# Moving a small gate's chain of work to an earlier stage, and storing residual rows to DRAM so that the last stage works in natural row order

## The chip, the cores and the metric

The kernel runs on one core of one Trainium2 chip. The metric is device time in microseconds (us) of one execution; the time of a kernel is the median of its runs. The engines are named as in the profile: PE (TensorE, matmuls), PEld (its weight loads, which overlap matmuls), DVE (VectorE), ACT (ScalarE), POOL (GpSimd), and SP (SyncE, which here only issues DMAs). Each engine works through its own instructions in order; semaphores order them against each other. "L208" is line 208 of the kernel.

## The reference

One layer of a streaming encoder over 512 rows ("tokens") of 1024 channels, in float32. Cut to what is computed:

```python
h = rms_norm(x, mix_norm_pre)
xa, ga, q, k, v, f_logit, g_a, g_b = split(h @ w_in)     # widths 1280 1280 1024 1024 1024 16 1024 1024
y_a = gelu(ga) * rg_lru(causal_dwconv4(xa))              # gated linear recurrence along the rows
cum = cumsum(log_sigmoid(f_logit + b_forget))            # the forget gate: one number per head and row
y_b = causal softmax(q k^T / 8 + cum_i - cum_j) @ v      # 16 heads of 64
merged = sigmoid(g_a + b0) * (y_a @ w_proj_a) + sigmoid(g_b + b1) * (y_b @ w_proj_b)
x = x + rms_norm(merged @ w_out, mix_norm_post)          # the residual rows
h = rms_norm(x, ffn_norm_pre)
u = causal_dwconv3(h @ w_up)                             # 6144 channels: gate and value halves
return x + rms_norm((gelu(u_gate) * u_val) @ w_down, ffn_norm_post)
```

The forget gate is a small part of it: 16 columns of the input projection, a log-sigmoid, and a running sum along the rows, of which the attention needs -8 times the sum as a bias for its keys.

## The kernel before

Every float32 operand of a matmul is split into a high part, rounded to the format in which PE multiplies at speed, and a low remainder; a product is three matmuls (high by high, high by low, low by high). So each weight tile of 128 partitions takes a DMA load into `raw`, a cast on ACT into `wh` (L205) and a subtraction on DVE into `wl` (L208). `raw`, `wh` and `wl` have four slots each. Activations are split in the same way.

The stages, in the order in which PE runs them, are: the projection xa with the gates of the recurrence; v in two halves (`v0`, `v1`, four weight tiles each); ga (ten tiles); pa, which multiplies the recurrent branch by w_proj_a in sixteen steps (L907 to L917); q0 and k0; the merge gates ma and mb, by a scheme with seven products in place of eight for a pair of tiles; the attention with the remaining q and k; pb; w_out (`wo`) with the two norms; the up projection by the same seven-product scheme; and the down projection by another one, in 42 steps of twelve matmuls.

What sets the order: a planner walks each engine's instructions by program order, and lets a later one go first where the earlier one isn't ready. `issue_after` ties instructions behind a named one on the same engine. Under `manual_schedule` (the gates, the up and down projections) the program's own order is kept. So v, ga, pa and the w_out stage are ordered by the planner, and the down projection by hand.

The pieces that the change touches, and those beside them:

- **The helper `background`** (L180): after each weight tile of the early stages, POOL copies one element of that weight into `tick` (L182) and then issues DMAs that prepare sums of the down weights. The copy reads `wh`, so that slot comes free only when the copy is done.
- **`forget`** (L836) is called in pa step 3 (L878). It loads w_f (L841), splits it on ACT and DVE (L844, L845), runs sixteen matmuls over all tokens into `pf` (L848, L849), and then works on 16 partitions by 512 columns: the copy of the low part (L851), the sum with the bias (L852), the log-sigmoid (`log1p_exp_neg`, L303: one Exp on ACT, then a series on DVE with seven multiply-adds at L315), the running sum (L860) and the scaled keys (L862). Four DMAs on SP's queue store the keys to the DRAM tile `cnd` (L864), from which the attention's bias is broadcast (L950). Its tiles come from the pool of the recurrence's `tt` tiles.
- **`early_sums`** (L876) is called after each pa step. From step 3 on the pools of the recurrence are closed; steps 6 to 11 compute sums of token halves `hf` (eight DVE operations of 128x1024, L887 to L893); step 12 loads the first pair of gate weights; steps 13 to 15 compute and split their sums (`gt`, `gth`, `gtl`).
- **The start of the gates** (L963 to L991): ACT casts the four `hf` into `gsh` (L967), DVE subtracts into `gsl`, then the weights of the first pair are split, the products p12 and p5 run, and `p.keep(2)` and `p.add` (L468, L480) have to be done before the next product.
- **The residual rows**: `x2t` holds x with 128 rows on partitions, 4 x 1024 values each. The host lays the rows of each block of 128 out so that the 64 even rows come first, then the 64 odd ones. `mix_norm` (L1225) adds the normed w_out output to `x2t` (L1240), squares it on ACT (L1242), takes the root (L270), scales it into `xn` (L1248) and hands it to PE for transposition (L294).
- **The down projection**: step i uses a weight tile (`wd[i]`) and a block of y, which `y_hi` (L1450) casts on ACT into `ah` and `y_lo` (L1456) subtracts on DVE into `al`. `tokens(..., parted)` reads every second column of y, and `placed` writes them side by side, so that the output rows come in the even-then-odd order of `x2t`. Later blocks of y are combined on DVE before (`q`, L1563). `prep(i)` is the order in which a step's four splits are issued; `extra` holds what is to be done beside a step.
- **The end**: blocks t = 2, 3 of the output are finished by a DMA that adds `x2t` (L1621), blocks 0 and 1 on DVE (L1615); the host reorders the rows of the result (L1784).

Of the kernel before, what the change touches and what calls it, by code (L numbers as in the profile page):

```python
# [8 lines left out]
F32 = mybir.dt.float32  # L9
# [3 lines left out]
ALU = mybir.AluOpType  # L13
# [84 lines left out]
def kernel(  # L98
# [432 lines left out]
    with ExitStack() as rg:  # L531
# [275 lines left out]

        v_out(0, pv)
        pv = v_start(1)
        for u in range(4):  # L810
            w = unit(f"v1_{u}")
            v_mm(u, pv, w)
            background(1, w)
            for t in range(5 * u // 2, 5 * (u + 1) // 2):
                batch([rg_tanh(t), rg_exp(t)])
                inflow(t)
        v_out(1, pv)
        steps = {0: (range(0, 4), ()), 1: (range(4, TR), range(0, 2)), 2: ((), range(2, 5)), 3: ((), range(5, 7)), 4: ((), range(7, 9)), 5: ((), range(9, TR))}
# [15 lines left out]
        cnd = ctx.enter_context(tc.tile_pool(name="cnd", bufs=1, space=bass.MemoryType.DRAM)).tile([H, PO[NT]], F32, name="cnd")  # L834

        def forget():  # L836
            def tl(name, n=H, dt=F32):
                return tpool.tile([P, S], dt, tag="tt", name=f"f_{name}")[0:n]

            fr = tl("fr", P)[:, : KD * H].rearrange("p (k e) -> p k e", k=KD)  # L840
            nc.sync.dma_start(fr, w_f)  # L841
            fw = tl("fw", P, F32R)[:, : KD * 48].rearrange("p (k e) -> p k e", k=KD)
            pool.memset(fw[:, :, H:32].bitcast(F32), 0.0)
            act.copy(fw[:, :, 0:H], fr)  # L844
            dve.tensor_tensor(out=fw[:, :, 32:48], in0=fr, in1=fw[:, :, 0:H].bitcast(F32), op=ALU.subtract)  # L845
            pf = bank("f")
            for k in range(KD):
                pe.matmul(pf[0:48], fw[:, k], turns(hh[:, k]), start=k == 0, stop=False)  # L848
                pe.matmul(pf[0:48], fw[:, k], turns(hl[:, k]), start=False, stop=k == KD - 1)  # L849
            z = tl("z")  # L850
            act.copy(z, pf[32:48])  # L851
            dve.scalar_tensor_tensor(out=z, in0=pf[0:H], scalar=cpt[0:H, C_BF : C_BF + 1], in1=z, op0=ALU.add, op1=ALU.add)  # L852
            with tc.issue_after(last_act[0].ins):
                l1p = log1p_exp_neg(z, tl)
            dve.tensor_scalar(out=z, in0=z, scalar1=0.0, scalar2=None, op0=ALU.min)
# [930 lines left out]
```

## Time and profile before

| | us |
|---|---|
| median of 3 runs | 884.94 (884.58 to 885.01) |
| the profiled execution | 884.92 |
| its span, first to last instruction | 883.1 |
| busy: PE, DVE, ACT, POOL | 868.6, 743.5, 608.4, 236.3 |

The profile is of one execution. Its span leaves out about 1.8 us around the first and last instruction. The granted clock of PE was 0.998 of full speed. Where the stages lie in the span, from the first matmul of each: ga from 126.5 us, pa from 178.3, q0 from 233.5, the gates from 245.0, the down projection from 760.0.

A row of the page's groups, or of the lines view, reads: line, engine, operation, output <- inputs, shapes, count | busy us, mean ns of one | idle time of the engine before it, and what ended that. A row of the timeline reads: start in us, duration, engine, line, operation, and in brackets the idle time before it and its releaser. A row of the waits view reads: who waited <- for whom: total us, how many times, the longest. A row of the windows view reads: stretch, its length, busy us of each engine shown with the number of instructions, the clock, the share of time that the DMA engines were busy, and GB/s. "q" behind an engine's name is its sequencer, which issues DMAs.

### The profile page before, as it was taken

Reading aid. Unit: us, or ns where it says so; the run is one execution under the profiler, and the core shown is the slowest. Engines: PE = TensorE matmul, PEld = TensorE weight load, DVE = VectorE, ACT = ScalarE, POOL = GpSimd, SP = SyncE. Lnnn points to the kernel's source line nnn. Section 1 sums busy time; section 2 is a strip of 40 time slices with the busy share of each in tenths; the row PEclk is TensorE's granted clock in tenths of the full one; section 3 lists DMA queues with packets and bytes.
Section 4 is the critical chain, followed back from the end, with each engine's and each line's share of the span. In section 5 each row is a group of like instructions: output and inputs, shape, how many; then the busy total and the mean of one; then the engine's idle time right before and its main releaser. Section 6 shows DMA issues by size and latency. Waiting matters only on the chain.

```text
span 883.1 us, 15782 instructions
## 1 busy us (share of the span) xinstructions
PE 868.6 (98%) x5856; PEld 792.3 (90%) x5856; DVE 743.5 (84%) x1209; ACT 608.4 (69%) x1031; POOL 236.3 (27%) x283
## 2 busy tenths in 40 slices
PE   9999999999999999999999999999999999999996
PEld 7888888888899998888888889999999999888884
DVE  8986479637978849998868599999999999889997
ACT  7565695532466648776754597888888888688774
POOL 4244344535411024232205100242332332100000
PEclk9999999999999999999999999999999999999999
DMA  7787689999865477453506762879899898699864
GB/s 269 242 288 207 188 214 265 227 273 196 190 148 165 120 261 274 133 173 127 203 26 203 234 200 95 192 178 241 210 222 240 209 233 210 230 384 303 280 192 147
DMA packets 71040, 185.24 MB, mean 210 GB/s; under 512 B 7153, under 2 KB 27681, under 8 KB 70578
## 3 DMA queue, kind: packets, MB, share of 16 engines
q1 hardware_dynamic: 47360, 127.72, 43.4%
q0 software_dynamic: 23456, 56.37, 29.8%
q8 instruction: 46, 0.75, 0.3%
q14 instruction: 32, 0.26, 0.1%
q10 hardware_dynamic: 146, 0.14, 0.0%
HBM read 150.69 MB, written 35.73 MB: 211 GB/s over the span
## 4 chain that ended last, share of the span: by engine, by line
PE 83%; DVE 8%; issue 4%; ACT 2%; POOL 2%; DMA 1%; DVEq 0%; ACTq 0%; POOLq 0%
PE up L464 7%; PE up L462 7%; PE up L461 7%; PE dn L1490 2%; PE dn L1488 2%; PE dn L1489 2%; PE ga L252 2%; PE ga L251 2%; PE ga L253 2%; DVE al L357 2%; PE pb L251 2%; PE xa L251 2%; PE v L341 2%; PE xa L253 2%; PE v L342 2%
## 5 line engine op out<-in xcount | busy, mean ns | idle before, releaser
L397 POOL DMA_DIRECT2D ml<-raw_up x42 | 36.1, 859 | 147.6 <-ACT ml L396 82.5
L1360 DVE SCALAR_TENSOR_TENSOR u<-up,cpt,u 128x511 f32<-128x511 f32 x96 | 71.3, 745 | 3.5 <-ACT u L1354 1.8
L1490 PE MATMUL dn<-wh_dn,al 128*128 128x512 f32 (+1 forms) x180 | 66.6, 370 | 1.3 <-DVE al L357 0.7
L1489 PE MATMUL dn<-wl_dn,ah 128*128 128x512 f32 (+1 forms) x180 | 66.1, 367 | 0.5 <-DVE wl_dn L208 0.5
L1488 PE MATMUL dn<-wh_dn,ah 128*128 128x512 f32 (+1 forms) x180 | 65.8, 366 | 0.2 <-ACT ah L1454 0.2
L461 PE MATMUL up<-sh,th 128*128 128x256 f32 x252 | 59.5, 275 | 0.0
L462 PE MATMUL up<-sl,th 128*128 128x256 f32 x252 | 59.5, 275 | 0.0
L208 DVE TENSOR_TENSOR wl_dn<-raw_dn,wh_dn 128x1024 fp32r<-128x1024 f32 x42 | 52.9, 1259 | 5.4 <-ACT wh_dn L205 5.2
L357 DVE TENSOR_TENSOR tl<-t,th 128x1024 fp32r<-128x1024 f32 x42 | 51.1, 1218 | 0.0
L1354 ACT ACTIVATE u<-up,cpt 128x512 f32<-128x512 f32 x48 | 37.0, 778 | 20.1 <-PE up L464 10.0
L205 ACT CAST wh_dn<-raw_dn 128x1024 fp32r<-128x1024 f32 x42 | 44.4, 1058 | 6.1 <-PE dn L1490 3.7
L461 PEld LDWEIGHTS up<-sh,th 128*128 128x128 f32 x252 | 48.4, 192 | 0.0
L462 PEld LDWEIGHTS up<-sl,th 128*128 128x128 f32 x252 | 48.4, 192 | 0.0
L1368 POOL TENSOR_TENSOR yf<-u,u 128x512 f32<-128x512 f32 x23 | 30.5, 1328 | 59.3 <-issue 46.5
L443 ACT CAST th<-t 128x1024 fp32r<-128x1024 f32 x42 | 43.8, 1044 | 2.4
L1490 PEld LDWEIGHTS dn<-wh_dn,al 128*128 128x128 f32 x180 | 34.1, 189 | 8.0 <-DVE al L357 4.1
L955 POOL TENSOR_TENSOR B<-B,mask 128x128 f32<-128x128 f32 x64 | 30.6, 506 | 34.8 <-DMA B<-cnd 33.7
L461 PE MATMUL up<-h2h,mh 128*128 128x256 f32 x168 | 39.7, 275 | 0.0
L462 PE MATMUL up<-h2l,mh 128*128 128x256 f32 x168 | 39.7, 275 | 0.0
L1489 PEld LDWEIGHTS dn<-wl_dn,ah 128*128 128x128 f32 x180 | 34.1, 189 | 5.8 <-DVE wl_dn L208 1.8
L1050 ACT ACTIVATE P<-P,mx 128x384 f32<-128x384 f32 (+3 forms) x64 | 35.2, 552 | 5.3 <-DVE mx L1045 4.3
L464 PE MATMUL up<-sh,tl 128*128 128x256 f32 x252 | 38.4, 275 | 0.0
(731 smaller groups left out, 3252.4 us busy)
## 6 DMA issues: line engine op xcount, KB each, us to landing
raw_up<-in_w_up_dram SPq DMA_DIRECT2D x48, 512.0 KB, 5.5
td<-in_w_down_dram POOLq DMA_DIRECT2D x36, 512.0 KB, 6.3
raw_dn<-td SPq DMA_DIRECT2D x24, 512.0 KB, 5.4
ml<-raw_up POOLq DMA_DIRECT2D x21, 512.0 KB, 5.4
B<-cnd POOLq DMA_DIRECT2D x16, 640.0 KB, 5.7
raw_dn<-in_w_down_dram SPq DMA_DIRECT2D x18, 512.0 KB, 4.4
raw_wo<-in_w_out_dram SPq DMA_DIRECT2D x16, 512.0 KB, 4.4
td<-td POOLq DMA_DIRECT2D x12, 512.0 KB, 11.2
```

The lines of the kernel that those rows point to most:

```text
L205: act.copy(self.wh, self.raw)
L208: engine.tensor_tensor(out=self.wl, in0=self.raw, in1=self.wh.bitcast(F32), op=ALU.subtract)
L251: pe.matmul(dst, ah, bh, start=first, stop=False)
L357: dve.tensor_tensor(out=out, in0=a, in1=b, op=ALU.subtract)
L443: act.copy(self.th[i], self.t[i])
L461: pe.matmul(dst, wh[:, k], turns(ah[:, k]), start=first and k == 0, stop=False, skip_group_check=True)
L462: pe.matmul(dst, wh[:, k], turns(al[:, k]), start=False, stop=False, skip_group_check=True)
L464: pe.matmul(dst, wl[:, k], turns(ah[:, k]), start=False, stop=k == KH - 1, skip_group_check=True)
L1360: dve.scalar_tensor_tensor(out=c[:, s:], in0=ps[:, : S - s], scalar=col(C_CFW + 3 * e + j), in1=c[:, s:], op0=ALU.mult, op1=ALU.add)
L1488: pe.matmul(d[:, x], ah[:, k, tok], bh, start=first, stop=False, skip_group_check=True)
L1489: pe.matmul(d[:, x], ah[:, k, tok], bl, start=False, stop=False, skip_group_check=True)
L1490: pe.matmul(d[:, x], al[:, k, tok], bh, start=False, stop=last, skip_group_check=True)
```

## The change

Three parts.

**1. The forget gate's chain moves from pa step 3 into the v1 stage.** `forget` becomes a generator with tiles of its own pool: before block 0 of v1 it loads and splits w_f; before block 2 it issues the sixteen matmuls; before block 3 the copy, the bias and the log-sigmoid; after the blocks the running sum and the four stores of keys. `early_sums` moves with it: the pools are closed in step 0, the eight `hf` operations go to steps 1 to 6 instead of 6 to 11, and the first pair of gate weights is loaded and summed one step earlier.

**2. The residual rows are stored.** When a block of `x2t` is complete, two DMAs on ACT's queue (64 partitions each) store it in natural row order to a DRAM tile `x2d`. In the down projection, beside steps 18 and 27, SP loads blocks 0 and 1 back into `x2t` in natural order, and the additions by DMA of blocks 2 and 3 read `x2d`.

**3. The down projection works in natural row order.** The splits of y lose their reordering, and the host its own at the end.

```diff
+        def forget():
+            def tl(name, n=H, dt=F32):
+                return fpool.tile([P, S], dt, name=f"f_{name}")[0:n]
+
+            fr = tl("fr", P)[:, : KD * H].rearrange("p (k e) -> p k e", k=KD)
+            nc.sync.dma_start(fr, w_f)
...
+            dve.tensor_tensor(out=fw[:, :, 32:48], in0=fr, in1=fw[:, :, 0:H].bitcast(F32), op=ALU.subtract)
+            yield
+            pf = bank("f")
+            for k in range(KD):
+                pe.matmul(pf[0:48], fw[:, k], turns(hh[:, k]), start=k == 0, stop=False)
+                pe.matmul(pf[0:48], fw[:, k], turns(hl[:, k]), start=False, stop=k == KD - 1)
+            z = tl("z")
+            yield
+            act.copy(z, pf[32:48])
...
+            with tc.issue_after(last_act[0].ins):
+                l1p = log1p_exp_neg(z, tl)
+            yield
...
+            for b in range(NT):
+                nc.sync.dma_start(cnd[:, PO[b] : PO[b + 1]], keys[:, : PO[b + 1] - PO[b]])
+
         v_out(0, pv)
         pv = v_start(1)
+        fstk0 = rg2.enter_context(ExitStack())
+        fpool = fstk0.enter_context(tc.tile_pool(name="forget", bufs=1, side="right", reuse_waits="tile"))
+        fg = forget()
         for u in range(4):
             w = unit(f"v1_{u}")
+            if u != 1:
+                next(fg, None)
             v_mm(u, pv, w)
             background(1, w)
             for t in range(5 * u // 2, 5 * (u + 1) // 2):
                 batch([rg_tanh(t), rg_exp(t)])
                 inflow(t)
+        next(fg, None)
         v_out(1, pv)
+        fstk0.close()
...
         def early_sums(step):
-            if step == 3:
-                forget()
+            if step == 0:
                 rg2.close()
...
-            elif 6 <= step < 10:
-                i = step - 6
+            elif step < 5:
+                i = step - 1
...
-            elif step == 10:
+            elif step == 5:
                 dve.tensor_tensor(out=fq[3], in0=fq[2], in1=fq[3], op=ALU.add)
                 sub(fq[2], fq[0], fq[2])
-            elif step == 11:
+            elif step == 6:
                 sub(fq[0], fq[3], fq[0])
                 sub(fq[1], fq[1], fq[0])
+            elif step == 11:
+                gp[0] = Pair(gates, 0, GP[0])
             elif step == 12:
-                gp[0] = Pair(gates, 0, GP[0])
-            elif step == 13:
                 gp[0].sums(0)
                 gp[0].sums(1)
...
+    x2n = x2d.rearrange("(t i a) d -> t a i d", a=2, i=HT)
+
+    def x2_out(t):
+        for a in range(2):
+            act.dma_start(x2n[t, a], x2t[HT * a : HT * (a + 1), t])
+
+    def x2_back(t):
+        nc.sync.dma_start(x2t[:, t], x2d[t * P : (t + 1) * P])
...
                 act.activation(out=xn[:, c], in_=x2t[:, t, c], func=AF.Square, accum_out=s3[:, i : i + 1])
+            x2_out(t)
             yield
...
-        act.copy(tokens(yhl[i][0], placed), tokens(yhl[i][2], parted))
+        act.copy(yhl[i][0], yhl[i][2])
...
-        sub(tokens(yhl[i][1], placed), tokens(yhl[i][2], parted), tokens(yhl[i][0].bitcast(F32), placed))
+        sub(yhl[i][1], yhl[i][2], yhl[i][0].bitcast(F32))
...
-            nc.gpsimd.dma_start(os[t], x2t[:, t], accum_op=ALU.add)
+            nc.gpsimd.dma_start(os[t], x2d[t * P : (t + 1) * P], accum_op=ALU.add)
...
+        for t in range(2):
+            extra[18 + 9 * t].append(lambda t=t: x2_back(t))
...
-    rows = r.results[0]["out_0_dram"].reshape(NT, 2, HT, D)
-    return rows.transpose(0, 2, 1, 3).reshape(1, S, D)
+    return r.results[0]["out_0_dram"][None]
```

45 lines of the change are left out of this document (14 added, 31 removed).

## The prediction

> **What bounds the kernel now.** I read the page's first lines, then the waits of the matmul engine and of its weight loads, then those waits stretch by stretch.
>
> ```profile
> span 883.1 us, 15782 instructions
> ...
> PE 868.6 (98%) x5856; PEld 792.3 (90%) x5856; DVE 743.5 (84%) x1209; ACT 608.4 (69%) x1031; POOL 236.3 (27%) x283
> ```
>
> PE is busy for 98% of the span. The change moves PE's work but takes none away, so only PE's waits and the tail behind its last matmul can be won. The waits (total, times, longest, in us), matmuls first, then weight loads:
>
> ```profile
> PE ma L461 <- DVE ma L480: 1.5, 1, 1.5
> PE q L253 <- DVE wl_q L208: 0.9, 1, 0.9
> ```
> ```profile
> PEld dn L1490 <- DVE al L357: 4.1, 9, 0.7
> ...
> PEld dn L1489 <- DVE wl_dn L208: 1.8, 4, 0.8
> ...
> PEld ma L461 <- DVE ma L480: 1.7, 1, 1.7
> ...
> PEld q L253 <- DVE wl_q L208: 1.3, 1, 1.3
> ```
>
> Matmuls are pipelined, so a wait costs between its PE and its PEld figure: 0.9 to 1.3 for q, 1.5 to 1.7 for ma. Both lie where the pa projection hands over to q, k and the gates. The dn waits lie at the two ends of the down projection, as its windows 755:785 (first fence) and 855:873 (second) say:
>
> ```profile
> PEld dn L1490 <- DVE al L357: 2.2, 5, 0.7
> ```
> ```profile
> PEld dn L1490 <- DVE al L357: 1.9, 4, 0.5
> ...
> PEld dn L1489 <- DVE wl_dn L208: 1.5, 3, 0.8
> ```
>
> So the change can win some 2.4 to 3.0 us at the handover, up to 2.2 at the start of the down projection and up to 3.4 at its end.
>
> **The handover.** These rows of the timeline (start, duration, engine) show why q and ma wait:
>
> ```profile
> 215.41 1.74 SPq L864 DMA_DIRECT2D cnd<-f_keys  x4
> 217.24 0.37 SPq L199 DMA_DIRECT2D raw_pa<-in_w_proj_a_dram  x1
> ```
> ```profile
> 221.47 4.63 DVE L887 TENSOR_TENSOR hf<-hh,hl 128x1024 f32<-128x1024 f32 x4 [2.52 <-DMA cnd<-f_keys]
> ...
> 233.71 1.22 DVE L208 TENSOR_TENSOR wl_q<-raw_q,wh_q 128x1024 fp32r<-128x1024 f32 x1
> ...
> 250.19 0.43 DVE L480 TENSOR_TENSOR ma<-ma,gx 128x256 f32<-128x256 f32 x1 [1.44 <-ACT gx L468]
> ```
> ```profile
> 229.04 8.20 POOL L182 COPY tick<-wh_pa 128x1 f32<-128x1 f32 x1
> ```
> ```profile
> 237.28 1.04 ACT L205 CAST wh_k<-raw_k 128x1024 fp32r<-128x1024 f32 x1 [2.33 <-POOL tick L182]
> ...
> 238.70 3.89 ACT L967 CAST gsh<-hf 128x1024 fp32r<-128x1024 f32 x4
> ```
>
> The forget gate's chain ends in four stores of keys on SP's queue; the last pa weights are issued behind them, at 217.24. The token sums hf wait until the stores have landed, at 221.47, and then fill DVE until wl_q goes at 233.71: that is q's wait. Meanwhile POOL's one-element copy takes 8.20 us, to 237.24; wh_k waits for it, gsh follows on the in-order ACT, and at the end of this train stands the addition of L480 at 250.19, for which ma waits.
>
> The change takes the chain out of this stretch and spreads the eight hf operations over pa steps 1 to 6, so no store stands before the last pa and q loads, and wl_q finds DVE free. **q: I take -1.1**, the middle of 0.9 and 1.3. wh_k needs a slot of the last pa weight, free when PE leaves pa, just before wl_q's start at 233.71, so gsh starts some 4 us sooner (about 234.6 instead of 238.70), more than ma's 1.7. **ma: -1.6**, bounds 0 and -1.7; what is late next is the same addition, with some 2 us in hand. The chain's Exp brings a table load:
>
> ```profile
> 195.48 1.28 ACT L306 ACT_TABLE_LOAD   x1
> ```
>
> In v1 the table with Exp is already there, and the gates' first Tanh must load it in its place. That lies between the copies gx and PE's next need of them, and ACT has gaps there: 0, at most +1.3.
>
> **The chain's new place.** PE's part, and DVE's in window 195.4:215.4 (everything, then L208 alone):
>
> ```profile
> L849 PE MATMUL f<-hl,f_fw x8: 379/379/379, 191.4 to 194.5; 128*48 128x512 f32 x8
> ```
> ```profile
> 195.40:215.40 20.00, 18.51 (x25) 1.00 0.93 189
> ```
> ```profile
> 195.40:215.40 20.00, 4.08 (x6) 1.00 0.93 189
> ```
>
> The sixteen f matmuls take 8 x 3.1/7 = 3.5 us here and 3.5 there: 0. DVE's part, 18.5 - 4.1 = 14.4 us, moves to the second half of v1 and into the ga projection. DVE's busy time in v1 and in two parts of ga, one ga weight split, and PE's ga matmuls:
>
> ```profile
> 105.70:126.50 20.80, 12.63 (x19) 1.00 0.73 181
> 126.50:157.00 30.50, 30.07 (x47) 1.00 1.06 284
> 157.00:182.30 25.30, 15.54 (x21) 1.00 1.00 249
> ```
> ```profile
> 155.62 1.24 DVE L208 TENSOR_TENSOR wl_ga<-raw_ga,wh_ga 128x1024 fp32r<-128x1024 f32 x1
> ```
> ```profile
> L251 PE MATMUL ga<-hh,wh_ga x80: 379/379/379, 126.5 to 177.6; 128*128 128x512 f32 x80
> ```
>
> A ga block takes 8 x 51.1/79 = 5.17 us, so ga7 starts at 162.7, and its split (155.62 + 1.24) is 5.9 us ahead: the thinnest lead by the splits' order. DVE has no room from 126.5 to 157 (0.4 us idle), 9.8 us after that. The f matmuls stand after two of v1's four blocks; behind them v1 leaves about 6/20.8 of its 8.2 us of idle DVE, 2.4, and PE comes 3.5 later. So DVE falls 14.4 - 2.4 - 3.5 = 8.5 us back. If wl_ga7 took its turn behind all of that, PE would wait 8.5 - 5.9 = 2.6. But the six L208 of the window just shown slipped in between links of this very chain, so a split that is ready need not queue behind the whole of it: **0, bounds 0 and +2.6**. DVE's 9.8 idle us take the backlog up before pa. Its other additions wait little: w_f's load stands on SP among ga weights that are fetched blocks ahead, and the key stores, which wait for the chain's end, now stand before ga and pa loads with the same lead; the two memsets on POOL stand before one-element copies whose weight slots are taken again only four weights later. The weights fw need load, cast and subtraction within v1's first two blocks, 10.3 us; if late, PE takes up to 2 us, inside the bound above.
>
> **The stores through ACT.** Eight stores of 64 rows, two behind each Square pair of L1242. Rows around the first norm, an ACT issue elsewhere, and PE's wait:
>
> ```profile
> 514.30 0.63 ACT L1242 ACTIVATE xn<-x2t 128x512 f32<-128x512 f32 x1
> ```
> ```profile
> 516.66 1.42 DVE L1248 SCALAR_TENSOR_TENSOR xn<-x2t,rs_f,gain 128x512 f32<-128x512 f32 x2
> ```
> ```profile
> 879.50 0.38 ACTq L1617 DMA_DIRECT2D out_dram<-o  x1
> ```
> ```profile
> PEld tr_f L294 <- DVE xn L1248: 0.3, 1, 0.3
> ```
>
> Behind a store wait the Squares of the next token block and then sd_f; DVE's xn waits for sd_f, and PE's transposes for xn, with no slack (0.3 us of wait today). Four issues stand before sd_f for blocks 0 and 1, and four again for 2 and 3: 4 x 0.38 = 1.5 each time if fully exposed, 3.0 in all. But an issue needs only x2t, as the Square of 0.63 before it does, and can go beside that Square. No row shows a DMA issue inside a busy stretch of ACT, so bounds 0 and +3.0; **I take +0.4**, near the hidden end. The load back of two blocks (SP, steps 18 and 27) is far ahead of its use, and the addition that now reads DRAM stands early in the tail: 0.
>
> **Natural order.** The split of y reads every second column today and afterwards reads straight through. Strided and plain operations of one size, ACT's and then a stretch of DVE's:
>
> ```profile
> L1454 ACT CAST ah<-q x36: 664/864/982, 776.2 to 866.4; 128x512 fp32r<-128x512 f32 x36
> ```
> ```profile
> L1292 ACT CAST sh<-hf x8: 614/620/626, 544.5 to 555.6; 128x512 fp32r<-128x512 f32 x8
> ```
> ```profile
> 827.51 1.22 DVE L208 TENSOR_TENSOR wl_dn<-raw_dn,wh_dn 128x1024 fp32r<-128x1024 f32 x1 [0.20 <-ACT wh_dn L205]
> 828.65 0.82 DVE L357 TENSOR_TENSOR al<-q,ah 128x512 fp32r<-128x512 f32 x1
> 829.39 0.68 DVE L1563 SCALAR_TENSOR_TENSOR q<-q,q 128x512 f32<-128x512 f32 x1
> 829.99 1.22 DVE L208 TENSOR_TENSOR wl_dn<-raw_dn,wh_dn 128x1024 fp32r<-128x1024 f32 x1
> ...
> 858.21 1.23 DVE L208 TENSOR_TENSOR wl_dn<-raw_dn,wh_dn 128x1024 fp32r<-128x1024 f32 x1 [1.62 <-ACT wh_dn L205]
> ...
> 878.32 1.54 DVE L1615 SCALAR_TENSOR_TENSOR o<-o,rs_o,x2t 128x512 f32<-128x512 f32 x3
> ```
>
> Start to start, al takes 0.74 and the plain q 0.60: 0.14 saved on DVE per step, 0.24 on ACT (864 - 620 ns). In mid-projection this only lengthens DVE's lead. Near the end the folds of the output are added to it, DVE falls behind, PE waits, and the tail to 878.32 + 1.54 is DVE's. 827.51 is the last start that waited for ACT before that, so from there the 16 remaining al count: 2.2 us at most; DVE's wait of 1.62 at 858.21 is for ACT, which itself follows DVE. **End: -1.7**, bounds 0 and -3.4 (PE's waits there). **Start: -0.3**, bounds 0 and -2.2: there al stands once behind each wait, and DMA landings set most of it.
>
> [...]
>
> **Sum**, against the profiled execution's own 884.92 us (span 883.1; the median of the runs is 884.94): -1.1 - 1.6 - 0.3 - 1.7 + 0.4 = -4.3, to 880.6; for small shifts in the order of the stages that were not ordered by hand I add 0.1: **880.7 us**, 0.48% faster.
>
> **Rivals.**
> - *The strided read is not what is slow* (something else in those rows, such as rows of 64, or y's own place). Then -1.7 and -0.3 go: 882.7. For it: al and ah also differ from the plain rows in where their input lies. Against: q, in the same place and stage, has 0.60. [...]
> - *ACT's issues are exposed.* +3.0 in place of +0.4: 883.3. For it: no slack at tr_f. Against: the Square beside them. Chance 0.15.
> - *A new wait at the handover*: ma still waits, since n's sums and ACT's casts stand before gx. 880.7 + 1.6 = 882.3. For it: that order is unchanged. Against: 4 us won before it. Chance 0.15.
> - *Slower: DVE without a gap in ga.* A POOL copy took 8.20 us, to 237.24, while DVE worked through hf and wl_q. ga's weight slots come free only through such a copy. With the chain in it, DVE has no gap from about 120 to 175; if a copy is then held as long, a slot is 8.2 late on top of the 2.6 of backlog: 880.7 + 2.6 + 8.2 = 891.5. It decides from the point where backlog plus copy exceed the lead of 5.9. For it: the row. Against: between 126.5 and 157 DVE is as full today, and no row of PE's waits names ga. Chance 0.14.
>
> **How the numbers follow.** Forecast 0.48 (879.5 to 882); the others as given. A measurement of this kernel can tell about 0.2% from no change, 1.77 us: faster is below 883.17, slower above 886.71. Faster: 0.48 + 0.08 + 0.15 + 0.03 of the second rival = 0.74; slower 0.14; same 0.12. The low end takes all bounds in favour, 884.92 - 1.3 - 1.7 - 3.4 = 878.5; the high end, 885.0, takes the exposed issues and most of the backlog, and leaves out the slower rival.
>
> **What would show it.** Right: no wait of PE q on wl_q and none of ma on L480; wh_k no longer behind a POOL copy; ah near 620 ns and al near 690; the dn waits at the end halved; the last DVE start nearer to the last matmul. Wrong: a wait of PE ga on wl_ga or wh_ga, POOL copies of several us in ga, a longer wait of tr_f on xn, a wait of f on f_fw, or ah still near 860 ns.

## The result and the profile after

The changed kernel took 897.16 us (median of 4 runs, 896.10 to 897.75), the kernel before 884.98 beside it (4 runs, 884.58 to 885.46). The ratio is 1.0136, with a 95% interval of 1.0119 to 1.0154: 12.2 us slower, where 880.7 us was forecast. Its profiled execution took 897.35 us with a span of 895.6.

The page's first lines of the changed kernel, then the waits of PE (total, times, longest):

```profile
span 895.6 us, 15806 instructions
...
PE 874.7 (98%) x5856; PEld 798.2 (89%) x5856; DVE 737.8 (82%) x1209; ACT 599.2 (67%) x1031; POOL 249.0 (28%) x283
```
```profile
PE k L251 <- ACT wh_k L205: 5.1, 1, 5.1
PE pa L253 <- DVE wl_pa L208: 2.6, 2, 2.4
...
PE tr_f L294 <- DVE xn L1269: 1.4, 1, 1.4
PE ga L253 <- DVE wl_ga L208: 1.0, 1, 1.0
```

The two waits that the change was to remove, q on wl_q and ma on L480, are no longer in the list. Four others stand in their place, and the longest belongs to k0, the stage between them. The waits of ga, pa and k add up to 8.7 us, less than the loss.

The next view shows where the work lies. From the first matmul of a stage in the trace to that of the next (the last two columns: to PE's last matmul, and from there to the last instruction), in us; pb to up is left out, since it took 93.2 to 93.5 in all of these. "Sums" counts the POOL issues of the down-weight sums (L160 and L163) between the first matmul of pa and that of the gates.

| kernel | v to ga | ga to pa | pa to gates | gates to pb | up to down | down | tail | sums |
|---|---|---|---|---|---|---|---|---|
| before | 50.12 | 51.80 | 66.74 | 191.57 | 230.20 | 115.62 | 7.49 | 12 |
| changed | 53.58 | 53.08 | 75.22 | 190.05 | 232.90 | 112.46 | 7.87 | 17 |
| e1, parts 2 and 3 | 50.12 | 51.80 | 66.69 | 191.80 | 232.11 | 113.05 | 7.50 | 12 |
| e2, forget gate in v1 alone | 53.58 | 53.11 | 74.95 | 190.17 | 230.24 | 114.93 | 7.49 | 16 |
| e3, no chain | 53.58 | 51.80 | 62.16 | 189.74 | 232.80 | 112.62 | 7.85 | 12 |
| e6, chain late | 53.58 | 51.80 | 62.16 | 191.49 | 232.11 | 112.91 | 7.90 | 13 |
| e7, sums moved | 53.57 | 53.11 | 63.51 | 197.66 | 232.79 | 112.98 | 7.76 | 0 |
| e11, part 3 alone | 50.12 | 51.80 | 66.70 | 191.48 | 230.35 | 112.53 | 7.49 | 12 |
| e12, stores by SP | 50.12 | 51.80 | 66.70 | 191.53 | 231.01 | 113.56 | 7.88 | 12 |
| e15, best | 53.58 | 51.80 | 62.16 | 190.92 | 231.04 | 112.55 | 7.80 | 13 |
| e16, sums crowded | 53.58 | 53.16 | 79.12 | 205.91 | 232.30 | 113.22 | 7.87 | 22 |

The sixteen f matmuls moved as expected: v to ga is 3.46 longer. Without them, pa to gates should be near 62.2, as in e3 and e6; it is 75.22. So while the spans are 12.4 us apart, 1.28 + (75.22 - 62.16) = 14.3 were lost in ga, pa, q0 and k0. The down projection gave back 3.16, and the up stage, where the stores were reckoned at 0.4, lost 2.70.

What happened in ga shows in the timeline of the changed kernel, POOL first, then ACT, then DVE (start, duration, and in brackets the idle time before it and its releaser):

```profile
144.20 28.77 POOL L182 COPY tick<-wh_ga 128x1 f32<-128x1 f32 x1 [3.90 <-ACT wh_ga L205]
172.91 2.04 POOL L163 DMA_DIRECT2D td<-td  x2
```
```profile
173.00 1.04 ACT L205 CAST wh_ga<-raw_ga 128x1024 fp32r<-128x1024 f32 x1 [3.54 <-POOL tick L182]
```
```profile
174.84 0.85 DVE L805 TENSOR_TENSOR yl<-gelu,yh 128x512 fp32r<-128x512 f32 x1 [1.92 <-ACT yh L804]
```

POOL's copy of one element per partition lasted 28.77 us. DVE was busy for all of that time (28.70 us with 34 operations in the window 144.2 to 172.9). The next weight cast needed the slot that this copy reads, so ACT stood for 3.54 us; then DVE, which waits for ACT, had nothing left to do, and in that gap POOL's copy came through. The three engines had tied a knot, and it came undone when DVE ran dry: DVE's gap begins at 172.92 us (174.84 - 1.92), and the copy ends at 172.97.

Behind the copy stand POOL's DMAs. The windows of the changed kernel (length, busy us of PE, PEld, DVE, ACT and POOL, the clock, the share of DMA time, GB/s), then two of the kernel before:

```profile
150.00:170.00 20.00, 20.00 (x95) 17.54 (x94) 20.00 (x25) 7.53 (x10) 20.00 (x1) 1.00 0.24 77
...
210.00:230.00 20.00, 20.00 (x94) 17.54 (x93) 7.36 (x10) 5.80 (x9) 5.79 (x8) 1.00 1.14 249
245.00:250.00 5.00, 0.58 (x3) 0.18 (x1) 0.20 (x1) 0.44 (x1) 1.20 (x2) 0.93 0.89 142
250.00:255.00 5.00, 4.30 (x9) 3.02 (x10) 4.16 (x4) 4.88 (x6) 0.00 (x0) 0.50 1.03 212
```
```profile
150.00:170.00 20.00, 20.00 (x94) 17.52 (x93) 16.32 (x21) 10.84 (x15) 9.51 (x12) 1.00 0.98 248
...
230.00:245.00 15.00, 14.14 (x66) 12.07 (x65) 13.64 (x14) 9.60 (x12) 7.24 (x1) 1.00 0.50 121
```

From 150 to 170 us the DMA engines were busy for 0.24 of the time instead of 0.98. What they did not do then, by this estimate (0.98 - 0.24) x 20 = 14.8 us of their time, came later: from 230 to 245 us their share is 1.17, against 0.50 in the kernel before, where the last sum was issued at 228.42. The end of that train is what k waited for:

```profile
241.67 1.01 POOL L163 DMA_DIRECT2D td<-td  x1 [5.25 <-DMA td<-td]
242.29 0.57 POOL L182 COPY tick<-wh_pa 128x1 f32<-128x1 f32 x1
248.33 1.01 POOL L163 DMA_DIRECT2D td<-td  x1 [5.46 <-DMA td<-td]
248.95 0.57 POOL L182 COPY tick<-wh_pa 128x1 f32<-128x1 f32 x1
```
```profile
249.56 1.04 ACT L205 CAST wh_k<-raw_k 128x1024 fp32r<-128x1024 f32 x1 [5.62 <-POOL tick L182]
```

Here the copies themselves are short. POOL waits over 5 us for the sum before, and the weight slot waits behind it. A wait of that length is not new; in the kernel before, the last sum waited as long, but it was issued 19.9 us earlier:

```profile
228.42 1.01 POOL L163 DMA_DIRECT2D td<-td  x1 [5.69 <-DMA td<-td]
```

So what changed is when the last sums go. After the idle of 5.1 us the granted clock is 0.50 for the next 5 us, and the k matmuls start 0.43 us apart there, against 0.22 from 256.22 us on. Behind pa's wait of 2.4 us it averaged 0.69 from 195 to 200 us. The clock adds to both of these waits.

### The profile page after: what moved, and what is told of

Its sections match the earlier page's. It is cut to its first block, busy times and chain, and to the rows that moved or that the text cites. A ratio compares the mean times of both kernels' runs of the same rounds, so it can differ in the third digit from the quotient of the medians.

```text
span 895.6 us, 15806 instructions
## 1 busy us (share of the span) xinstructions
PE 874.7 (98%) x5856; PEld 798.2 (89%) x5856; DVE 737.8 (82%) x1209; ACT 599.2 (67%) x1031; POOL 249.0 (28%) x283
## 4 chain that ended last, share of the span: by engine, by line
PE 70%; DVE 10%; issue 6%; ACT 5%; DMA 5%; POOL 4%; ACTq 0%; DVEq 0%; SPq 0%; POOLq 0%
PE up L462 7%; PE up L464 7%; PE up L461 7%; POOL tick L182 3%; DMA td<-td 3%; PE dn L1508 2%; PE dn L1506 2%; PE dn L1507 2%; PE pb L251 2%; PE xa L251 2%; PE xa L253 2%; PE xa L252 2%; PE pb L252 2%; PE pb L253 1%; DVE al L357 1%
## 5 line engine op out<-in xcount | busy, mean ns | idle before, releaser
L182 POOL COPY tick<-wh_ga 128x1 f32<-128x1 f32 x10 | 42.3, 4229 | 22.6 <-ACT wh_ga L205 22.6
```

What stands on the lines that cost most here:

```text
L182: i = pool.tensor_copy(out=tick, in_=w[0].bitcast(F32)[:, 0, 0:1])
```

## The experiments

Theory A: the chain on DVE, behind v1, makes DVE late in ga, POOL's copy is held, and the sums and slots behind it come late (A1), or the weight loads lose their lead (A2). Rivals: the token sums moved to pa's first steps (B), and SP standing at the key stores (S). "Before" is the kernel before, timed beside each run. Diffs are against the changed kernel unless it is said otherwise, and cut to the lines that matter.

### e1: parts 2 and 3 alone

The `forget` and `early_sums` of the kernel before; the rest as changed.

> Parts 2 and 3 alone: the forget gate and the token sums as before, the residual rows stored through ACT and the down projection in natural order. Every theory on part 1 gives the same here, since part 1 is not in it: the down projection's waits fall from 5.0 to 2.0 us as in the changed kernel (-3.0), ACT's issues before sd_f cost +0.9, so about 882.9 us (881.5 to 884). Near 897 would mean that part 1 is not what costs.

884.66 us against 885.02, ratio 0.9993 (0.9983 to 1.0003), above the 881.5 to 884 expected. The down projection won 2.57 us, and the up stage lost 1.91. So parts 2 and 3 nearly cancel, and part 1 costs all of the loss.

### e2: the forget gate in v1 alone

```diff
-            if step == 0:
+            if step == 3:
                 rg2.close()
...
-            elif step < 5:
-                i = step - 1
+            elif 6 <= step < 10:
+                i = step - 6
```

Parts 2 and 3 are not in it.

> The forget gate in v1 alone: token sums at the old steps (pools closed in step 3, hf in steps 6 to 11, the pair in 12 to 15), parts 2 and 3 not in it. Theory A (the chain leaves DVE without a gap in ga, POOL's one-element copy is held some 29 us, the down-weight sums and the weight slots come late): the copy is held over 15 us again, PE waits on wh_k or wh_q, 891 to 897 us. Theory B (the token sums moved to pa's first steps are what costs, the chain in v1 is harmless): 882 to 885.5 us, no wait of PE on wh_k over 1 us.

895.83 us, ratio 1.0119 (1.0102 to 1.0136). The copy is held again, and k waits 5.2 us:

```profile
143.65 28.84 POOL L182 COPY tick<-wh_ga 128x1 f32<-128x1 f32 x1 [3.92 <-ACT wh_ga L205]
```

B falls: the place of the token sums hardly matters.

### e3: the chain's DVE work left out

```diff
-            with tc.issue_after(last_act[0].ins):
-                l1p = log1p_exp_neg(z, tl)
             yield
-            dve.tensor_scalar(out=z, in0=z, scalar1=0.0, scalar2=None, op0=ALU.min)
...
-            dve.tensor_scalar(out=placed(keys), in0=parted(cum), scalar1=-8.0, scalar2=None, op0=ALU.mult)
+            dve.tensor_scalar(out=placed(keys), in0=parted(z), scalar1=-8.0, scalar2=None, op0=ALU.mult)
```

> The changed kernel with the log-sigmoid and the running sum left out: the keys are the scaled logits, so 16 of the chain's DVE operations and the Exp are gone, while w_f's load and split, the sixteen matmuls, the four stores and the moved token sums stay. Theory A: no POOL copy over 6 us in ga, wh_k's slot in time, 881 to 885 us. Theory B (moved token sums) and theory S (the stores and w_f's load on SP): 894 to 898 us, the wait of PE on wh_k stays near 5 us.

881.89 us, ratio 0.9966 (0.9953 to 0.9979): the loss is gone, and k's wait with it. The surprise is how little DVE's busy time in ga differs. The window 126 to 180, of e3 and then of the changed kernel, and POOL's copies of ga weights in it:

```profile
126.00:180.00 54.00, 54.00 (x252) 47.29 (x251) 50.93 (x70) 30.08 (x55) 20.31 (x28) 1.00 1.00 238
```
```profile
126.00:180.00 54.00, 52.99 (x246) 46.19 (x245) 51.90 (x75) 28.40 (x51) 41.40 (x19) 1.00 0.62 149
```
```profile
L182 POOL COPY tick<-wh_ga 128x1 f32<-128x1 f32 x8 | 6.4, 803 | 31.2 <-ACT wh_ga L205 31.2
```
```profile
L182 POOL COPY tick<-wh_ga 128x1 f32<-128x1 f32 x7 | 37.9, 5418 | 14.5 <-ACT wh_ga L205 14.5
```

DVE is busy for 50.93 of 54 us without the chain and 51.90 with it, since e3's token sums are drawn forward into the free time. The copies take 803 ns on average in the one and 5418 in the other. A share of busy time does not tell the two apart. What does is how far DVE runs behind its inputs: from the third ga weight on, the split on DVE (`wl_ga`) starts 0.6 to 3.0 us after the cast on ACT that it needs (`wh_ga`) has ended in e3, and 2.2 to 12.1 us after it in the changed kernel.

### e4: weight slots that don't wait for POOL

```diff
+            if self.pace:
+                self.tk = cpool.tile([P, 1], F32, tag="tk", name="tk_" + self.pace, bufs=8)
+                act.copy(self.tk, self.raw[:, 0:1])
...
-        i = pool.tensor_copy(out=tick, in_=w[0].bitcast(F32)[:, 0, 0:1])
+        i = pool.tensor_copy(out=tick, in_=w[2] if len(w) > 2 else w[0].bitcast(F32)[:, 0, 0:1])
```

> The changed kernel, but POOL's one-element copy reads a small tile that ACT fills beside each weight cast (a 128x1 copy on ACT more per tile of v1, ga and pa), so a weight slot no longer waits for POOL. The copy itself is still held and the down-weight sums still come late. Theory A1 (the cost goes through the weight slots): ACT's waits on tick and PE's wait on wh_k vanish, 885 to 889 us. Theory A2 (the cost is the late sums' DMA traffic, weights landing late): 893 to 898 us.

914.81 us, ratio 1.0334 (1.0319 to 1.0350), worse than any theory had. The copy was held for 30.47 us again; no slot waited for POOL, but from 190 us on ACT waited for the weights themselves (23.1 us in the changed kernel):

```profile
ACT tk_pa L209 <- DMA raw_pa<-in_w_proj_a_dram: 51.5, 12, 9.6
```

So slots behind POOL need not be the whole of it: with them out of the way, the late sums seem to meet pa's own loads. The small copies on ACT also lengthened v and shifted the order there (v to ga 61.51), so the size of this run says nothing, and it decides nothing between A1 and A2.

### e5: the key stores later

```diff
             dve.tensor_scalar(out=placed(keys), in0=parted(cum), scalar1=-8.0, scalar2=None, op0=ALU.mult)
+            yield
             for b in range(NT):
...
             background(2, w)
+            if t == 5:
+                next(fg, None)
```

> The changed kernel, but the four key stores are issued in ga block 5 instead of right behind v1, so SP never stands at a store whose keys are not there yet (it stood 19.2 us in the changed kernel). DVE's chain stays where it is. Theory S (the loads of ga and pa behind the waiting stores are what costs): raw_ga is issued near 125 to 133 us again, 882 to 887 us. Theory A (DVE's order itself: no low part of a ga weight is made while the chain runs, so no raw slot comes free, and POOL's copy is held): still 893 to 898 us, raw_ga issued after 141 us as before.

896.25 us, ratio 1.0138 (1.0121 to 1.0156). As a test of S it missed: the planner drew the stores forward again, to the moment the keys were ready, and SP stood for 19.2 us as before. But its order of SP's issues is instructive:

```profile
141.11 1.31 SPq L842 DMA_DIRECT2D cnd<-f_keys  x3
142.53 1.63 SPq L199 DMA_DIRECT2D raw_ga<-in_w_in_dram  x2
144.21 0.47 SPq L842 DMA_DIRECT2D cnd<-f_keys  x1
```

The loads go at 142.53, which is when the `wl_ga` that started at 141.01 (1.2 us) leaves a raw slot free. They could not have gone before, stores or none. Against S speaks e7, which keeps SP's wait of 19.2 us and loses little from ga to the gates.

### e6: the chain late in ga

```diff
+            yield
             with tc.issue_after(last_act[0].ins):
                 l1p = log1p_exp_neg(z, tl)
...
-        next(fg, None)
         v_out(1, pv)
-        fstk0.close()
...
                 gate_out(i)
+            if t in (7, 9):
+                next(fg, None)
```

> The changed kernel with the log-sigmoid, the running sum and the stores issued at ga blocks 7 and 9 instead of at the end of v1 (the sixteen matmuls and the bias stay in v1). DVE then has the chain where it idles, not ahead of the ga splits. Theory A: POOL copies under 6 us in ga, no wait of PE on wh_k over 1 us, 881 to 886 us. Theory S would expect the same gain only if SP's wait at the stores falls too. If the sixteen matmuls in v1 or the moved token sums cost by themselves: 890 or more.

884.11 us, ratio 0.9999 (0.9988 to 1.0010). ga to pa and pa to gates are what they are without any chain, with all of its work done; the longest copy is 4.44 us, behind a pa weight. So neither the matmuls in v1 nor the moved sums cost anything in these stretches: it is the chain's place on DVE. SP's wait at the stores fell too, to 2.1 us, so e6 alone does not tell this from S. PE still waits 1.0 us for ma on L480.

### e7 and e16: the sums taken away, or crowded

e7:

```diff
-            background(2, w)
+            if t < 3:
+                background(2, w)
...
-            background(1, (wh, wl))
...
             nc.gpsimd.dma_start(B, cnd[h : h + 1, :].partition_broadcast(P))
+            for _ in range(2):
+                next(transfers, lambda: None)()
```

> The changed kernel, but from ga block 3 to the end of pa POOL makes no one-element copies and issues no down-weight sums; the remaining 29 transfers are issued beside the bias loads of the attention. DVE's chain and SP's stores stay as in the changed kernel. Theory A1 (what costs is POOL's copy held 28.8 us, and the weight slots and sums behind it): 882 to 888 us, PE's wait on wh_k gone; whatever the late sums cost in attention comes on top. Theory A2 (what costs is that no ga weight is split while the chain runs, so the loads lose their lead): PE still loses 5 us or more in pa and k, 891 to 898 us.

904.00 us, ratio 1.0225 (1.0207 to 1.0244). The whole misleads here. The planner also orders POOL's DMAs, and it drew 16 of the moved transfers to the time before ga (35 there instead of 19), where the kernel lost 9.5 us before its first v matmul; 8 more stood in the gates and the attention, which took 7.6 us longer. What the run was for is the stretch between: no sum in pa, and pa to gates takes 63.51 us, 1.35 over e6 instead of 13.06, though the chain, SP's wait and the late splits of ga stay. PE's waits from ga to the gates:

```profile
PE pa L253 <- DVE wl_pa L208: 1.1, 1, 1.1
PE ga L253 <- DVE wl_ga L208: 1.0, 1, 1.0
```

That is what A2 is worth by itself: some 2.7 us (1.31 in ga, 1.35 behind), not 14.3. But e7 also took away the sums that pa has in the kernel before, 12 of them; what the lost lead costs beside those, no run shows.

e16 was to be the clean form, with pa's own sums left alone:

```diff
-            background(2, w)
+            if t < 3:
+                background(2, w)
...
+            next(transfers, lambda: None)()
```

> The changed kernel without POOL's copies and sums from ga block 3 to ga block 9; these 14 transfers are issued beside the attention's bias loads (one per load), while pa keeps its own copy and sum per step. The chain, SP's stores and the late splitting of the ga weights stay, and pa's traffic is that of the kernel before. Theory A1 (the held copy, which pushes ga's sums into pa): from the first ga matmul to the first of the gates 114 to 119 us, no wait of PE on wh_k over 1 us. Theory A2 (the loads' lost lead alone): 123 us or more there, with PE's waits in pa and on wh_k. The whole time also holds what the moved transfers cost in the attention.

917.13 us, ratio 1.0370 (1.0340 to 1.0400), and again not what was meant: the planner put the moved transfers into pa, 22 of them up to the gates instead of 17. So it became the opposite of e7, and tells the other half. No copy is held (the longest is 3.88 us), yet pa to gates is 79.12 us, and PE waits where the changed kernel waited, and for q too:

```profile
PE k L251 <- ACT wh_k L205: 5.1, 1, 5.1
PE q L251 <- ACT wh_q L205: 4.3, 1, 4.3
```

The ga splits are late in both runs. With no sums in pa little is lost (e7); with 22 of them much is lost, though no copy is held (e16). In the changed kernel the held copy is what puts the sums there.

### e9 and e14: DVE made to wait for POOL

```diff
             background(2, w)
+            dve.tensor_copy(out=seen, in_=tick)
```

> The changed kernel with one more DVE operation per ga block: a 128x1 copy that reads POOL's tick, so DVE itself waits until POOL's one-element copy has been let through. The chain stays where it is, and so does the late splitting of the ga weights; only POOL's long hold is taken away, for ten operations of some 0.1 to 0.2 us each and the waits at them. Theory A1 (POOL's held copy, and the sums and slots behind it, are the cost): no copy over 3 us in ga, the time from the first ga matmul to the first of the gates falls from 128.3 us to 115 to 119, the whole to 884 to 889 us. Theory A2 (the loads' lost lead is the cost): that stretch stays at 125 us or more, 893 to 898 us.

892.37 us, ratio 1.0082 (1.0056 to 1.0108), between the theories. The copy was held for 7.52 us only, but POOL had to stand for DVE to read the last tick, which lay behind the chain:

```profile
148.80 7.52 POOL L183 COPY tick<-wh_ga 128x1 f32<-128x1 f32 x1 [17.99 <-DVE seen L868]
```

e14 gives each copy a tile of its own:

```diff
-        i = pool.tensor_copy(out=tick, in_=w[0].bitcast(F32)[:, 0, 0:1])
+        ticks.append(cpool.tile([P, 1], F32, tag="tick", name=f"tick{len(ticks)}", bufs=16))
+        i = pool.tensor_copy(out=ticks[-1], in_=w[0].bitcast(F32)[:, 0, 0:1])
```

> As e9, but each of POOL's copies has a tile of its own, so POOL no longer waits for DVE to have read the last one (it did so for 18.0 us in e9); DVE still waits at its 128x1 copy until POOL's copy is through. Theory A1 (the held copy and the sums behind it are the cost): no copy over 8 us in ga, no idle of POOL over 8 us before it, from the first ga matmul to the first of the gates 115 to 120 us, the whole 884 to 890 us. Theory A2 (the loads' lost lead): that stretch stays above 122 us, 891 us or more.

894.17 us, ratio 1.0107 (1.0094 to 1.0121), pa to gates 71.78. It missed its purpose: the hold is 25.51 us. DVE's read of this copy stood behind so much other work that it was no help. From ga to the gates e9 takes 123.27 us and e14 125.03, against 113.96 in e6 and 128.30 in the changed kernel. In both, POOL's sums still come some 25 us late: in e14 through the hold, in e9 through the wait of 17.99 us and the hold behind it. So neither took away what A1 names, and though e14's times lie where A2 was expected, the two decide nothing.

### e10 and e13: what in the chain holds the copy

e10 takes one operation out, the reciprocal; e13 puts plain work of the chain's amount in its place:

```diff
-        dve.reciprocal(d, d)
+        if recip:
+            dve.reciprocal(d, d)
```
```diff
-            with tc.issue_after(last_act[0].ins):
-                l1p = log1p_exp_neg(z, tl)
+            fill = tl("fill")
+            for _ in range(12):
+                dve.scalar_tensor_tensor(out=fill, in0=z, scalar=1.0, in1=z, op0=ALU.mult, op1=ALU.max)
...
```

The same twelve operations stand once more in place of the running sum.

> The changed kernel with the reciprocal of the log-sigmoid left out, one operation of 3.34 us of the chain's 14.4; all its other links stay. If the amount of the chain's work decides (DVE catches up 3.3 us sooner and finds a gap in ga): the hold of POOL's copy ends some 5 to 15 us earlier and the time falls to 885 to 893 us. If the hold comes from this one operation (DVE's operations overlap by 0.07 us instead of 0.08 from it on, until the first gap): no copy over 6 us in ga, 881 to 885 us. If neither: 894 to 897 us.

> The chain's log-sigmoid and running sum left out as in e3, and 24 operations on DVE of 16 x 512 put in their place that depend on nothing but the biased logits (about 24 x 0.6 = 14.4 us, the chain's own amount). If the amount of DVE work ahead of the ga splits decides (DVE falls behind its inputs, and POOL's copy is held until it runs dry): a copy held over 15 us in ga, 891 to 898 us. If it is something in the chain's own operations (the wait of each link for the one before, the running sum, the Exp): no hold over 6 us, 882 to 886 us.

e10: 896.97 us, ratio 1.0130 (1.0109 to 1.0150). With 3.34 us less work the hold is 28.44 us, as long as before. e13: 896.41 us, ratio 1.0133 (1.0119 to 1.0147):

```profile
157.41 26.12 POOL L182 COPY tick<-wh_ga 128x1 f32<-128x1 f32 x1 [8.23 <-ACT wh_ga L205]
```

So it is not something in the chain's own operations: plain DVE work of the same amount at that place does it too. And the length of the hold doesn't follow the amount of work: 28.44 us with 3.34 us less of it. In the changed kernel it lasts until DVE runs dry, which comes when ACT stands for the slot behind the copy; in e13 DVE is as busy beside the hold, 20.00 of the 20 us from 150 to 170.

e10 also speaks for A1 against A2. Without the reciprocal the ga splits start at most 7.1 us after their casts, instead of 12.1, and ga takes no more than its 51.80 us. Yet with a hold as long, pa to gates takes 76.49 us, of which PE waits 9.9 for wh_k: from ga to the gates 128.29 us, as in the changed kernel.

### e8, e11 and e12: what parts 2 and 3 cost and bring

Against the kernel of e1, e8 issues the stores behind xn, e11 leaves stores and loads back out, and e12 gives the stores to SP:

```diff
-            x2_out(t)
             yield
...
+            x2_out(t)
             yield
             turned[t] = to_channels(xn, t, h2h, h2l, hf, "f")
```
```diff
-            nc.gpsimd.dma_start(os[t], x2d[t * P : (t + 1) * P], accum_op=ALU.add)
+            nc.gpsimd.dma_start(os[t], x2t[:, t], accum_op=ALU.add)
```
```diff
-            act.dma_start(x2n[t, a], x2t[HT * a : HT * (a + 1), t])
+            nc.sync.dma_start(x2n[t, a], x2t[HT * a : HT * (a + 1), t])
```

> Parts 2 and 3 alone as in e1, but ACT issues the two stores of a block behind sd_f and xn of that block instead of ahead of them. If ACT's issues ahead of sd_f are what ate the down projection's gain: the stalls between 520 and 560 us fall from 4.7 back to about 3.0 us, and the time from 884.66 to 882.2 to 883.5 us. If the stores cost by their traffic or not at all: no change, 884 to 885 us.

> Part 3 alone: the down projection in natural order on the kernel before, with no store and no load back of the residual rows; the last addition then adds residual rows in the other order. If the stores through ACT cost what the up stage lost (230.2 us before, 232.1 in e1): up is back at 230.2 to 230.5, the down projection at 112.5 to 113, the whole 881.5 to 883 us. If the order of y is what shifts the up stage: 884 to 885 us.

> Parts 2 and 3 alone as in e1, but the stores are issued by SP in place of ACT. If ACT's issue time is the cost: the up stage falls from 232.1 to 230.2 to 230.8 us, the whole to 882 to 883.3 us. If the stores' traffic against the up weights is the cost, or the loads queued behind the stores on SP are held: 884 us or more.

e8: 886.24 us, ratio 1.0018 (1.0006 to 1.0030), no gain. Up to down stays at 232.24: the planner put a third `wl_up` ahead of the second xn, and so gave away what ACT had won. e11: 882.77 us, ratio 0.9974 (0.9964 to 0.9985): natural order alone wins 2.0 us, and the up stage is back at 230.35. e12: 883.48 us, ratio 0.9988 (0.9979 to 0.9997), up to down 231.01. So the stores cost 1.8 us in the up stage through ACT and 0.7 through SP. Why, ACT's timeline of the changed kernel shows:

```profile
547.66 0.63 ACT L1262 ACTIVATE xn<-x2t 128x512 f32<-128x512 f32 x1
547.72 1.10 ACTq L1212 DMA_DIRECT2D x2d<-x2t  x2
548.20 0.19 ACT L1262 ACTIVATION_READ_ACCUMULATOR xn<-x2t 128x1 f32 x1
549.21 0.63 ACT L1262 ACTIVATE xn<-x2t 128x512 f32<-128x512 f32 x1 [0.82 <-DVE ss_f L1266]
```

The two issues take 1.10 us where two at 0.38 were reckoned; they begin beside a Square of 0.63 but end after it, and the next Square starts after 0.82 us of idle time. Its bracket names DVE's ss_f, which ended at 548.96; but in the kernel before the same Square began 0.5 us ahead of ss_f, so it does not need it. With SP issuing, in e12, the Squares follow each other at once, and PE's wait for xn at tr_f is 0.2 us, against 1.3 in e1:

```profile
535.67 0.63 ACT L1252 ACTIVATE xn<-x2t 128x512 f32<-128x512 f32 x1
...
536.34 0.63 ACT L1252 ACTIVATE xn<-x2t 128x512 f32<-128x512 f32 x1
```

### e15: the parts that won

e6 and e12 together.

> The chain issued at ga blocks 7 and 9 as in e6, and the residual rows stored through SP as in e12. If the two gains add up (e6 won 1.1 us from v to the gates, e12 won 1.3 us against before with what it left in the down projection): 882 to 883.5 us, faster than both kernels.

883.23 us against 884.75 (12 runs and 17), ratio 0.9988 (0.9977 to 0.9999): some 1.5% below the changed kernel and barely below the one before. It has the short pa to gates of e6 (62.16), the down projection at 112.55, and no copy over 4.34 us.

## Why the prediction was wrong

**The step that failed is "The chain's new place": 0, bounds 0 and +2.6.** It measured +14.3 (1.28 in ga, 13.06 from pa to the gates, against e6). It counted DVE's time and the lead of the splits, and trusted that "a split that is ready need not queue behind the whole of it". On the chip the chain did stand ahead of them, as DVE's rows of the changed kernel show:

```profile
120.56 1.23 DVE L208 TENSOR_TENSOR wl_ga<-raw_ga,wh_ga 128x1024 fp32r<-128x1024 f32 x1 [0.78 <-ACT wh_ga L205]
...
141.22 1.21 DVE L208 TENSOR_TENSOR wl_ga<-raw_ga,wh_ga 128x1024 fp32r<-128x1024 f32 x1
```

No ga weight was split for 20 us. Yet by itself that lateness was worth only some 2.7 us (e7, with no sums in pa), near the bound given. The rest came through POOL: its other work in this stretch was dismissed with "whose weight slots are taken again only four weights later", and its DMAs were not reckoned as work with a date.

**The slower rival named the mechanism and mis-sized it.** "DVE without a gap in ga", at 0.14, was priced as one hold of 8.2 us on top of 2.6, to 891.5. The hold was 28.77. It asked only when a slot comes free; what decided was that the DMA engines were idle for some 14.8 us more of their time, so that the sums fell into the handover, and that the clock fell to 0.50 behind the wait of 5.1 us. The argument against it, that DVE is as full there today, was true and worthless: e3 is as full (50.93 of 54 us) and holds nothing. What differs is how far DVE is behind its inputs: its ga splits start up to 12.1 us after their casts in the changed kernel and 7.1 in e10, which hold a copy, and at most 3.0 in e3.

**q -1.1 and ma -1.6.** Both waits went. v to the gates is 167.54 us in e6 against 168.66 before, -1.1, as q's term said; ma's gain shows in the changed kernel in the stretch behind (gates to pb 190.05 against 191.57), but there by luck: k's wait delays the gates, and L480 is done in that time. In e6, without the delay, ma still waits 1.0 us, so of that 1.6 a clean form keeps little: the third rival, at 0.15, was right there.

**Stores through ACT, +0.4 with bounds 0 and +3.0.** 1.8 us (e1 less e11) and 2.7 in the changed kernel: the second rival. The taken value assumed that the issues hide beside a Square; the pair, at 1.10 us, is longer than the Square of 0.63. The changed kernel's figure also holds a clock of 0.83 for the 10 us around the wait at tr_f; in e1 it is 1.00 there.

**Natural order, -2.0.** Right in cause and nearly in size: the down stage won 3.16 us in the changed kernel, and part 3 alone 2.0 in the whole. The end won what was taken, 1.7; the start, put at 0.3, won 1.4: after a fifth of the stage's matmuls the changed kernel is that much ahead. The count of 16 al behind the end's value overlooks a DVE start at 855.84 us that waited 0.36 us for ACT, so the fit does not prove the count. The rows after, ACT's split and DVE's:

```profile
L1472 ACT CAST ah<-q 128x512 fp32r<-128x512 f32 x36 | 22.2, 618 | 1.6 <-DVE q L1581 0.9 <-DVE q L357 0.6
```
```profile
L357 DVE TENSOR_TENSOR al<-q,ah 128x512 fp32r<-128x512 f32 x36 | 24.8, 690 | 0.0
```

864 ns became 618 and 690 is what was forecast for al. Part 3 takes away the step of two and the rows of 64 together. That it is the step, a row of the kernel before says, where ACT steps by two in rows of 256 and is as slow:

```profile
L804 ACT CAST yh<-gelu x10: 815/870/881, 140.5 to 180.5; 128x512 fp32r<-128x512 f32 x10
```

So the first rival, whose 0.08 stands in the sum of the chances, falls: a cast on ACT that steps by two took 864 and 870 ns in these rows, a straight one 618. The tail behind PE's last matmul did not shorten, 7.87 us against 7.49: PE ended sooner, and DVE's last work is as long as it was.

**The clock** was no term at all. pa and k waited 7.7 us in all, but the stretch lost 13.06; of the difference of 5.4, the clock gives some 4.6 by an estimate from three stretches of 5 us: 2.5 and 0.55 behind k's wait (0.50 from 250 us, 0.89 from 255), and 1.55 behind pa's (0.69 from 195).

**The table load** was forecast for the gates' first Tanh. In the changed kernel it came at the attention's first Exp (L1060, 1.28 us at 336.6); PE shows no wait there.

**The range.** The high end, 885.0, left the slower rival out, as it says. With it in, 891.5, the range would still have missed 897.16: no row of the trace before bounds how long a copy can be held. The low end, 878.5, claims all bounds in favour but leaves out the 2.2 at the start of the down projection; with it, 876.3.

## What to carry to other kernels

Before moving work to a full engine, ask whether that engine then runs behind its inputs, not how busy it is: here 51 of 54 busy us were harmless and 52 cost 14 us. Follow the moved work to the engines whose own work stands until it pauses (here POOL's copy, for 28.77 us), and to the transfers that these engines issue: here a sum that was issued at 172.91 us, where e3 issued it at 146.11, came out as PE's wait at the next handover. And price a PE wait of some us with the slower clock behind it (here 0.50 for 5 us behind 5.1 us, 0.69 behind 2.4).

## What the runs showed of the hardware

**A one-element copy on POOL lasted 26 to 29 us**: 28.77, 28.84, 28.44 and 26.12 in four kernels (the changed one, e2, e10, e13). In the changed kernel DVE made no pause in that time, 28.70 busy us of 28.70 with 34 operations, all of them with two inputs in SBUF, and the copy came through between none of them. In e3 DVE also has a stretch without idle time, and POOL's copies there took 0.54, 1.06 and 1.11 us:

```profile
135.00:156.00 21.00, 21.00 (x99) 18.39 (x98) 21.00 (x28) 9.86 (x17) 8.43 (x11) 1.00 1.03 238
```
```profile
145.12 1.06 POOL L182 COPY tick<-wh_ga 128x1 f32<-128x1 f32 x1 [3.42 <-ACT wh_ga L205]
```

What lets POOL in between two operations there and not in the changed kernel stays open. DVE far behind its inputs (12.1 us in the changed kernel, 3.0 in e3) goes with the hold, but it is not enough: in the changed kernel at 137.77 us, with no ga weight split since 121.79, a copy took 0.18 us, beside a DVE operation that reads one of its inputs from PSUM (L352, 0.27 us at 137.72). In e13 a copy at 142.63 took 0.18 us too, before the one that was held from 157.41.

**The clock fell after waits of 1.4 to 5.1 us.** After 5.1 us without matmuls it was granted at 0.50 for 5 us, after pa's wait of 2.4 us it averaged 0.69 over 5, and after the wait of 1.4 us at tr_f 0.83 over the window of 10 that holds it:

```profile
550.00:560.00 10.00, 8.48 (x78) 7.92 (x78) 9.27 (x15) 5.15 (x12) 0.00 (x0) 0.83 0.58 191
```

In e1 a wait of 1.3 us at the same place left it at 1.00. So these runs do not show how long a wait has to be: 1.4 us was followed by a lower clock in the one, 1.3 by none in the other.
